# Two ranked expert lists with If/Else arms, two dense blocks, and one-hots with two tokens innermost

## The chip, the core and the metric

One core of a Trainium2 chip runs the whole program. The metric is the device time of one execution in microseconds; a kernel's time is the median of its runs.

## The reference

Two layers of a network on 256 tokens of width 2048 (an S5 mixer, sparse attention, then a block with two linear-attention mixers), and at the end the part that matters here, a layer of 16,384 small experts. Each token picks, for each of 8 heads, the 16 best experts; every expert e has a row u_e and a row v_e of 2048 numbers:

```python
expert = i1 * 128 + i2                      # 8 heads x 16 picks for a token
gate = softmax(best)                        # over the 16 of a head
hid = gelu(sum_d x[t, d] * u[expert, d])
y[t] = sum over the 128 picks of gate * hid * v[expert]
h = h + y; out = rmsnorm(h) * final_norm_g
```

## The kernel before

Everything below is in `peer`, the last stage, and the generators that it drives, `gates` and `sort`. Tokens are two halves of 128, t = 0 and 1. An expert's index is n1 * 128 + p: n1 is one of 128 blocks, p a partition. The kernel computes the hidden value of all experts for all tokens, multiplies it by a gate that is zero where a token did not pick the expert, and multiplies only those experts by v that some token picked.

**The `pu` loop.** For each n1, 48 matmuls of 128 x 256 give the 128 experts' hidden values for 256 tokens (`mm_b`, line 212). The weights come in two units of 512 KB for each n1; ACT rounds a unit to its high part (`wh`, line 152) and DVE takes the rest (`wl`, line 153), three units ahead. A gelu (line 1741) and a DMA on ACT's queue write 128 rows of `WG` in memory (line 1742); a row of `WG` holds one expert's 256 hidden values, then its 256 gates.

**`gates`** runs through a hook between the matmuls of that loop, from n1 = 32. For four tokens at a time (`build`), DVE makes one-hots: `gA` (which p), `gE` (which n1) and `gB` (gE times the three bf16 parts of the gate). Sixteen bf16 matmuls of 128 columns turn them into gates (`pg`, line 1529) and into counts for each expert and half (`cnt`, line 1530). ACT copies the result to `gst`, and every 64 tokens 8 DMAs from ACT's queue write the gates to `WG` (line 1536). **`sort`** follows through the same hook: it classes each expert as picked in both halves, the first only, the second only, or neither, gives each a position in this order by prefix sums, and turns the positions into a list of expert numbers, again with one-hots and matmuls of 256 columns (`pL`, line 1615). The list lies as `idx`, 128 positions of 128 experts; `cuts` holds the ends of the classes in positions.

**The visits** (lines 1777 to 1811). 128 positions are taken in an order fixed by hand. A position is guarded by registers that hold the cuts: what lies behind the end is skipped by every engine. In a visit POOL gathers 128 rows of v (`vraw`, 1 MB, line 1721) and 128 rows of `WG` (`wg`, 256 KB, line 1729) by indirect DMA, each in a guard of its own, up to four and three visits ahead. POOL multiplies hidden value and gate (`hm`, line 1786), ACT rounds (`hh`, `vwh`, lines 1787 and 1789), DVE takes the rests (`hlo`, `vwl`, lines 1788 and 1790). TensorE adds three products of such parts to the 2048 output columns of a half, 12 matmuls of 512 columns for each half that the position serves (`mm`, line 1799): one half for the classes first and second, two for both. Zero matmuls (line 1774) clear the accumulators beforehand. The tile framework orders each engine's instructions, so a call that stands later in the text can stand earlier on an engine.

The **final norm** (lines 1814 to 1829) adds the accumulators to h on DVE, squares on ACT, takes the root on POOL (line 606), scales and writes out.

Of the kernel before, what the change touches and what calls it, by code (L numbers as in the profile page):

```python
# [169 lines left out]
class Kern:  # L170
# [1325 lines left out]
    def gates(self, P, RT, G, cnt):  # L1496
# [7 lines left out]
        def build(b):  # L1504
            ts = slice(b * nt, (b + 1) * nt)
            A = P.tile([128, 128, nt], BF16, name="gA", bufs=2)
            E = P.tile([128, 128, nt], BF16, name="gE", bufs=2)
            B = P.tile([128, 3, 128, nt], BF16, name="gB", bufs=2)
            bc = lambda n: RT[:, n, None, ts].to_broadcast([128, 128, nt])
            v.tensor_tensor(A, self.iota4, bc(1), op=OP.is_equal)  # L1510
            v.tensor_tensor(E, self.iota4, bc(0), op=OP.is_equal)
            v.tensor_tensor(B, E[:, None, :, :].to_broadcast([128, 3, 128, nt]),
                            RT[:, 2:5, None, ts].to_broadcast([128, 3, 128, nt]), op=OP.mult)
            AB[b] = A, E, B

        build(0)
        yield 1
        for b in range(T // nt):
# [4 lines left out]
            if b * nt % ng == 0:  # L1523
                st = self.stage.tile([128, 128, ng], F32, name="gst", bufs=2)
            ps = self.psum.tile([128, nt, 128], F32, tag="g", name="pg", bufs=2)
            half, first, last = b * nt // 128, b * nt % 128 == 0, (b + 1) * nt % 128 == 0
            for j in range(nt):
                for n in range(3):
                    pe.matmul(ps[:, j, :], A[:, :, j], B[:, n, :, j], start=(n == 0), stop=(n == 2))
                pe.matmul(cnt[:, half, :], A[:, :, j], E[:, :, j], start=(first and j == 0), stop=(last and j == nt - 1))  # L1530
            o = b * nt % ng
            act.activation(st[:, :, o:o + nt], ps.rearrange("p t n -> p n t"), AF.Copy)
            if o + nt == ng:
                for n in range(0, 128, 16):
                    t0 = b * nt + nt - ng
                    nc.scalar.dma_start(G[n * 128:(n + 16) * 128, t0:t0 + ng].rearrange("(n p) t -> p n t", p=128),
                                        st[:, n:n + 16, :])
            yield 1

    def sort(self, P, cnt, idx, cuts):  # L1540
# [7 lines left out]
        v.tensor_scalar(m, cnt, 1.0, None, op0=OP.min)  # L1548
        I = tl([4, 128], "sI")
# [3 lines left out]
        v.tensor_scalar(I[:, 3], m[:, 0], -1.0, 1.0, op0=OP.mult, op1=OP.add)  # L1553
        yield 1
        S = tl([4, 128], "sS")
        fl = lambda x: x.rearrange("p a b -> p (a b)")
        v.tensor_tensor_scan(fl(S), fl(self.smask), fl(I), 0.0, op0=OP.mult, op1=OP.add)
        R = tl([4], "sR")
        v.tensor_copy(R, S[:, :, 127])
        ps = self.psum.tile([128, 2, 4], F32, tag="g", name="psr", bufs=2)  # L1560
# [3 lines left out]
        tot, cum, off = tl([4], "stot"), tl([4], "scum"), tl([4], "soff")  # L1564
        v.tensor_copy(tot, ps[:, 1])
        v.tensor_tensor_scan(cum, self.ones[:, 0:4], tot, 0.0, op0=OP.mult, op1=OP.add)
        v.tensor_tensor(off, cum, tot, op=OP.subtract)
        v.tensor_tensor(off, off, ps[:, 0], op=OP.add)
        v.tensor_scalar(off, off, -1.0, None, op0=OP.add)
        ci = tl([4], "sci", I32)  # L1570
        v.tensor_copy(ci[:, 0:3], cum[:, 0:3])
        v.tensor_copy(ci[:, 3:4], cum[:, 2:3])
        v.tensor_scalar(cuts[:, 0:2], ci[:, 0:2], 127, None, op0=OP.add)
        v.tensor_copy(cuts[:, 2:3], ci[:, 1:2])
        v.tensor_scalar(cuts[:, 3:4], ci[:, 3:4], 127, None, op0=OP.add)
        v.tensor_scalar(cuts, cuts, 7, None, op0=OP.arith_shift_right)
        yield 1
        for c in range(4):
            v.scalar_tensor_tensor(S[:, c], S[:, c], off[:, c:c + 1], I[:, c], op0=OP.add, op1=OP.mult)
        pos = tl([128], "spos")  # L1580
        v.tensor_reduce(pos, S.rearrange("p c n -> p n c"), axis=AX.X, op=OP.add)
# [13 lines left out]
        def build(b):  # L1595
            ts = slice(b * nt, (b + 1) * nt)
            A = P.tile([128, 128, nt], BF16, name="gA", bufs=2)
            E = P.tile([128, 128, nt], BF16, name="gE", bufs=2)
            B = P.tile([128, 3, 128, nt], BF16, name="gB", bufs=2)
            for o, a in ((A, 0), (E, 1)):  # L1600
                v.tensor_tensor(o, self.iota4, pb[:, a, None, ts].to_broadcast([128, 128, nt]), op=OP.is_equal)
            v.tensor_tensor(B[:, 0:2], E[:, None, :, :].to_broadcast([128, 2, 128, nt]),
                            self.nv[:, :, None, ts].to_broadcast([128, 2, 128, nt]), op=OP.mult)
            AB[b] = A, B
# [12 lines left out]
        Ls = tl([2, 128], "sL")  # L1617
        v.tensor_copy(Ls, L)
        v.scalar_tensor_tensor(idx, Ls[:, 0], 128.0, Ls[:, 1], op0=OP.mult, op1=OP.add)
        yield 1  # L1620

    def peer(self, keep, M, mixR, g1):
# [63 lines left out]
        self.iota4 = rt([128, 4], "iota4", BF16)  # L1686
        v.tensor_copy(self.iota4, ib[:, :, None].to_broadcast([128, 128, 4]))
        self.srt, self.ones, self.smask = rt([129], "srt"), rt([128], "ones"), rt([4, 128], "smask")
# [3 lines left out]
        v.tensor_copy(self.nv[:, 1], self.srt[:, 128:129].to_broadcast([128, 128]))  # L1692
        gp.memset(self.ones, 1.0)
        gp.memset(self.smask, 1.0)
        gp.memset(self.smask[:, :, 0:1], 0.0)
# [3 lines left out]
        idx = rt([128], "idx", U32)  # L1699
        cuts = rt([4], "cuts", I32)  # L1700
        WG = self.dram.tile([16384, 2 * T], F32, name="WG")
        left, stage = ExitStack(), ExitStack()
        NR, NS, NV = 32, 78, 54
        reg = {}

        def regs():
            for k, n, engines in (("both", 0, (ET.PE,)), ("first", 1, (ET.PE,)), ("second", 2, (ET.PE,)),
                                  ("end", 3, (ET.PE,)), ("load", 3, (ET.Pool,)),
                                  ("split", 3, (ET.Activation, ET.DVE, ET.Pool))):
                reg[k] = nc.values_load(cuts[0:1, n:n + 1], engines=engines, min_val=0, max_val=128)  # L1710


        order = [j for n in range(NV) for j in (n, n + NV)] + list(range(2 * NV, 128))
        raw, wg, hl = {}, {}, {}

        def gather_v(q):
            if q < 128:
                j = order[q]
# [5 lines left out]
        def gather_w(q):  # L1724
            if q < 128:
                j = order[q]
                wg[q] = vr.tile([128, 2, T], F32, name="wg", bufs=4)
                with tc.If(reg["load"] > j):
# [4 lines left out]
        for n in range(128):  # L1733
# [17 lines left out]
            elif n == 123:  # L1751
                self.finish()
                regs()
                for q in range(4):
                    gather_v(q)
# [14 lines left out]
        for q in range(3):  # L1770
            gather_w(q)
# [118 lines left out]
```

## Time and profile before

| | |
|---|---|
| median of 3 runs | 3229.49 us (3229.22 to 3232.59) |
| profiled execution: its own time, its span | 3227.61 us, 3225.7 us |
| mean granted TensorE clock | 0.958 of full speed |
| TensorE, DVE, ACT, POOL busy | 91%, 59%, 43%, 21% |
| `pu` matmuls, line 212, x6144 | 758.0 + 583.5 us busy |
| products of the visits, line 1799, x1920 | 257.9 + 252.8 + 251.3 us busy |
| gathers on POOL, x109 each | 178.8 us (`wg`) and 171.3 us (`vraw`) |
| hm on POOL, hlo and vwl on DVE | x109 each; vwl 249.6 us |

The busy times of matmuls overlap, so the time of a product is read from starts. The page's chain of waits breaks off at POOL's queue near the end; what stands there is read from the timeline and the waits. The stages of the whole: other layers until 1669 us, the `pu` loop to 2606, the visits to 3125, the final norm to 3225.7.

### The profile page before, as it was taken

To read this page: it belongs to the slowest core of one execution; us is meant where nothing else is said; L and a number is where in the kernel's file an instruction comes from. 1 tells how busy PE (TensorE), PEld (TensorE's weight loads), DVE (VectorE), ACT (ScalarE), POOL (GpSimd) and SP (SyncE) were. 2 spreads that over 40 slices of the span, in tenths; PEclk is the share of its full clock that TensorE was granted. 3 is DMA by queue.
4 is the path that set the end of the run, shared out by engine and by line. 5 is a ranking of instruction groups with operands and counts; after the bars stand their busy time and mean duration, and the time that the engine had idled before them with its cause. 6 is when DMAs were issued, how large, how long until landed. Compare 5 with 4: busy or idle time off the path is not lost. (4 is left out here: it accounts for less than half of the span.)

```text
span 3225.7 us, 51109 instructions
## 1 busy us (share of the span) xinstructions
PE 2944.7 (91%) x19491; PEld 2668.9 (83%) x19496; DVE 1895.3 (59%) x2632; ACT 1376.7 (43%) x1806; POOL 677.7 (21%) x502
## 2 busy tenths in 40 slices
PE   7888999999997999899999999999899989999950
PEld 6887899888787999788899999999799967777740
DVE  8858544555567663575689855555654445555540
ACT  4464333444445573444434433334234434444430
POOL 4443000000001000310001100000000048878840
PEclk9889999999998999999999999999899999999985
DMA  4244645444564553236656656655666668878840
GB/s 166 66 143 160 215 165 176 138 144 142 172 224 145 174 158 107 69 113 221 193 174 194 197 154 177 176 157 155 178 221 207 206 216 292 292 277 283 288 162 26
DMA packets 216662, 574.38 MB, mean 178 GB/s; under 512 B 84240, under 2 KB 101776, under 8 KB 200144
## 3 DMA queue, kind: packets, MB, share of 16 engines
q1 hardware_dynamic: 106928, 392.32, 37.8%
q0 software_dynamic: 24416, 142.88, 12.4%
q10 hardware_dynamic: 85056, 35.66, 4.0%
q8 instruction: 167, 2.74, 0.3%
q14 instruction: 95, 0.78, 0.1%
HBM read 530.95 MB, written 39.85 MB: 177 GB/s over the span
## 5 line engine op out<-in xcount | busy, mean ns | idle before, releaser
L153 DVE TENSOR_TENSOR wl<-raw,wh 128x1024 fp32r<-128x1024 f32 x685 | 885.8, 1296 | 790.3 <-ACT wh L152 785.7
L152 ACT ACTIVATE wh<-raw 128x1024 fp32r<-128x1024 f32 x688 | 728.7, 1060 | 1156.0 <-PE pu L212 385.0
L212 PE MATMUL pu<-h,wh 128*128 128x256 f32 x4096 | 758.0, 286 | 6.8 <-ACT wh L152 5.5
L212 PEld LDWEIGHTS pu<-h,wh 128*128 128x128 f32 x4096 | 641.9, 191 | 10.0 <-ACT wh L152 5.9
L212 PE MATMUL pu<-h,wl 128*128 128x256 f32 x2048 | 583.5, 285 | 5.4 <-DVE wl L153 5.1
L212 PEld LDWEIGHTS pu<-h,wl 128*128 128x128 f32 x2048 | 388.0, 189 | 8.2 <-DVE wl L153 8.1
L227 PE MATMUL pz<-wh,t 128*128 128x512 f32 x1024 | 336.0, 400 | 0.0
L1790 DVE TENSOR_TENSOR vwl<-vraw,vwh 128x2048 fp32r<-128x2048 f32 x109 | 249.6, 2290 | 103.6 <-ACT vwh L1789 103.6
L1799 PE MATMUL acc<-vwh,hh 128*128 128x512 f32 x640 | 257.9, 403 | 57.1 <-PEq L1807 18.8
L1799 PE MATMUL acc<-vwh,hlo 128*128 128x512 f32 x640 | 252.8, 395 | 0.0
L1799 PE MATMUL acc<-vwl,hh 128*128 128x512 f32 x640 | 251.3, 393 | 0.0
L1729 POOL DMA_INDIRECT wg<-WG,idx x109 | 178.8, 1640 | 259.0 <-DMA WG<-w 233.6
L227 PEld LDWEIGHTS pz<-wh,t 128*128 128x128 f32 x1024 | 192.4, 188 | 40.7 <-issue 1.0
L1789 ACT ACTIVATE vwh<-vraw 128x2048 fp32r<-128x2048 f32 x109 | 208.3, 1911 | 18.4 <-PE acc L1799 11.7
L1799 PEld LDWEIGHTS acc<-vwh,hh 128*128 128x128 f32 x640 | 121.0, 189 | 107.0 <-ACT hh L1787 46.0
L227 PE MATMUL pz<-wl,t 128*128 128x512 f32 x512 | 201.2, 393 | 1.6 <-DVE wl L153 1.4
L227 PE MATMUL pso<-wh,t 128*128 128x512 f32 x640 | 200.6, 393 | 0.3 <-DVE th L986 0.3
L1721 POOL DMA_INDIRECT vraw<-pv,idx x109 | 171.3, 1571 | 136.7 <-PE pu L212 96.0
L1787 ACT ACTIVATE hh<-hm 128x256 fp32r<-128x256 f32 x109 | 44.6, 409 | 253.2 <-POOL hm L1786 253.2
L1799 PEld LDWEIGHTS acc<-vwh,hlo 128*128 128x128 f32 x640 | 121.1, 189 | 30.7 <-DVE hlo L1788 5.3
L227 PEld LDWEIGHTS pso<-wh,t 128*128 128x128 f32 x640 | 120.2, 188 | 27.1 <-DVE th L986 0.7
L1799 PEld LDWEIGHTS acc<-vwl,hh 128*128 128x128 f32 x640 | 121.2, 189 | 23.0
(601 smaller groups left out, 5150.5 us busy)
## 6 DMA issues: line engine op xcount, KB each, us to landing
raw<-pu SPq DMA_DIRECT2D x256, 512.0 KB, 3.8
raw<-w_z SPq DMA_DIRECT2D x96, 512.0 KB, 3.4
raw<-w_fqi SPq DMA_DIRECT2D x48, 512.0 KB, 3.5
raw<-w_a_in SPq DMA_DIRECT2D x32, 512.0 KB, 3.5
raw<-w_q SPq DMA_DIRECT2D x32, 512.0 KB, 3.4
raw<-w_b_out SPq DMA_DIRECT2D x32, 512.0 KB, 4.0
raw<-w_conv SPq DMA_DIRECT2D x32, 512.0 KB, 3.7
raw<-w_gz SPq DMA_DIRECT2D x32, 512.0 KB, 3.4
```

The source lines that it names most:

```text
L152: self.nc.scalar.activation(h, t, AF.Copy)
L153: m = (engine or self.nc.vector).tensor_tensor(l, t, h.bitcast(F32), op=OP.subtract).ins
L212: mm = nc.tensor.matmul(ps, a[:, c], b(k), start=(k == 0 and n == 0), stop=(k == nk - 1 and n == len(ops) - 1))
L227: self.nc.tensor.matmul(pss[tt], x[a](k)[:, ts], b[:, kk * 512:(kk + 1) * 512], start=(k == 0 and n == 0), stop=(k == nk - 1 and n == 2))
L1721: gp.indirect_dma_start(out=raw[q], out_offset=None, in_=i["pv"], in_offset=bass.IndirectOffsetOnAxis(ap=idx[:, j:j + 1], axis=0))
L1729: gp.indirect_dma_start(out=wg[q].rearrange("p a t -> p (a t)"), out_offset=None, in_=WG[:, :], in_offset=bass.IndirectOffsetOnAxis(ap=idx ...
L1787: act.activation(hh, hm, AF.Copy)
L1789: act.activation(wh, r, AF.Copy)
L1790: v.tensor_tensor(wl, r, wh.bitcast(F32), op=OP.subtract)
L1799: pe.matmul(acc[t][e], a[:, ts], b[:, es], start=False, stop=True, skip_group_check=True)
```

## The change

`gates` and `sort` hold one-hots as [2 groups, 128, 2 tokens] instead of [128, 4 tokens], so a matmul reads every second element instead of every fourth; gB is built by two DVE instructions instead of one. `sort` makes two lists. List 1 (a = 0) holds the experts of both halves, then those of the first only; list 2 (a = 1) holds those of the second only, its chunks numbered on from the end of class both or from position 44, whichever is later. A position n is one visit: the list-1 chunk serves the first half; then an If/Else adds to the second half either the same chunk (class both) or list 2's chunk n. Positions 0 to 81 are taken in a merged order of the first 50 and the other 32; a second loop over the rest stands behind a guard that is true only if a list is longer than 82 positions. List 2 gathers only the second half of a row of `WG`, which now holds [half, hidden or gate, 128 tokens] behind one row of zeros. The last two n1 blocks (126, 127) are left out of the lists: their v rows are loaded whole at n1 = 118 and 119, and each is multiplied for both halves; the first of them starts the accumulators in place of the zero matmuls. Both gathers of a job stand in one guard, three jobs ahead; `hm` is on DVE; `vraw` has 3 buffers instead of 4. The registers are read at n1 = 116 instead of 123.

The diff, cut to what moves work (`self.split` is the ACT copy and the DVE subtraction of the visits):

```diff
 def gates
+    def hot(self, P, name, vals, parts=1):
+        o = P.tile([128, 2, 128, 2], BF16, name=name, bufs=2)
+        self.nc.vector.tensor_tensor(o, self.iota2[:, None, :, :].to_broadcast([128, 2, 128, 2]),
+                                     vals.rearrange("p (g i) -> p g i", i=2)[:, :, None, :].to_broadcast([128, 2, 128, 2]),
+                                     op=OP.is_equal)
+        return o
...
-            v.tensor_tensor(A, self.iota4, bc(1), op=OP.is_equal)
-            v.tensor_tensor(E, self.iota4, bc(0), op=OP.is_equal)
-            v.tensor_tensor(B, E[:, None, :, :].to_broadcast([128, 3, 128, nt]),
-                            RT[:, 2:5, None, ts].to_broadcast([128, 3, 128, nt]), op=OP.mult)
+            A, E = self.hot(P, "gA", RT[:, 1, ts]), self.hot(P, "gE", RT[:, 0, ts])
+            B = P.tile([128, 3, 2, 128, 2], BF16, name="gB", bufs=2)
+            for g in range(2):
+                tg = slice(b * nt + 2 * g, b * nt + 2 * g + 2)
+                v.tensor_tensor(B[:, :, g], E[:, None, g].to_broadcast([128, 3, 128, 2]),
+                                RT[:, 2:5, None, tg].to_broadcast([128, 3, 128, 2]), op=OP.mult)
...
-                    pe.matmul(ps[:, j, :], A[:, :, j], B[:, n, :, j], start=(n == 0), stop=(n == 2))
+                    pe.matmul(ps[:, j, :], A[:, g, :, k], B[:, n, g, :, k], start=(n == 0), stop=(n == 2))
...
-                for n in range(0, 128, 16):
+                for n in range(0, nn, nn // 7):
...
+                nc.scalar.dma_start(GD[:, half, t0:t0 + ng].rearrange("(n p) t -> p n t", p=128), st[:, nn:128, :])
 def sort
-                pe.matmul(L, A[:, :, j], B[:, 0:2, :, j], start=(b + j == 0), stop=(b == nb - 1 and j == nt - 1))
+                pe.matmul(L, A[:, g, :, k], B[:, 0:2, g, :, k], start=(b + j == 0), stop=(b == nb - 1 and j == nt - 1))
 def peer
+        NR, ND, NQ0, NM = 32, 2, 44, 82
...
-        order = [j for n in range(NV) for j in (n, n + NV)] + list(range(2 * NV, 128))
+        order = sorted(range(NM), key=lambda n: (n + 0.5) / 50 if n < 50 else (n - 49.5) / (NM - 50))
...
+        def cond(r, a, n):
+            both, first, second = reg[r]
+            return (first > n) if a == 0 else (both <= n) & (second > n)
+
+        def jobs(ns):
+            return [(a, n) for n in ns for a in range(2) if (n >= NQ0 if a else n < 128)]
...
-                raw[q] = vr.tile([128, D], F32, name="vraw", bufs=4)
-                with tc.If(reg["load"] > j):
-                    gp.indirect_dma_start(out=raw[q], out_offset=None, in_=i["pv"],
-                                          in_offset=bass.IndirectOffsetOnAxis(ap=idx[:, j:j + 1], axis=0))
+            r = raw[job] = vr.tile([128, D], F32, name="vraw", bufs=3)
+            g = wg[job] = vr.tile([128, 2 - a, 2, 128], F32, name=f"wg{a}", bufs=3)
...
+            with tc.If(cond("load", a, n)):
+                gp.indirect_dma_start(out=g.rearrange("p a b t -> p (a b t)"), out_offset=None,
+                                      in_=wghalf if a else wgrows, in_offset=off(0))
+                gp.indirect_dma_start(out=r, out_offset=None, in_=i["pv"], in_offset=off(1))
...
-                gp.tensor_tensor(hm, g[:, 0], g[:, 1], op=OP.mult)
+            with tc.If(cond("split", a, n)):
+                v.tensor_tensor(h, g[:, :, 0], g[:, :, 1], op=OP.mult)
...
+            with tc.If(first > n):
+                mm(w[0], 0)
+            with tc.If(both > n) as c:
+                mm(w[0], 1, 1)
+            if 1 in w:
+                with c.Else():
+                    with tc.If(second > n):
+                        mm(w[1], 1)
...
+                for x, (f, ahead) in enumerate(((gather, 3), (gate, 2), (prep, 1))):
...
-            nc.scalar.dma_start(WG[n * 128:(n + 1) * 128, 0:T], w)
+            if n < nn:
+                nc.scalar.dma_start(WG[1 + n * 128:129 + n * 128, :, 0, :], w)
+            else:
+                wh, wl, hh, hlo, g = dense[n]
+                h = vs.tile([128, 2, 128], F32, name="hm0", bufs=3)
+                v.tensor_tensor(h, w, g, op=OP.mult)
+                self.split(hh, hlo, h)
...
+            elif 118 <= n < 118 + ND:
+                m = nn + n - 118
+                r = vr.tile([128, D], F32, name="vraw", bufs=3)
+                nc.sync.dma_start(r, i["pv"][m * 128:(m + 1) * 128])
...
+                self.split(wh, wl, r)
...
-        for t in range(2):
-            for e in range(4):
-                pe.matmul(acc[t][e], z[:, 0:128], z, start=True, stop=True)
+        for n in range(nn, 128):
+            for t in range(2):
+                mm(dense[n][0:4], t, t, n == nn)
+        run(order)
+        with tc.If(reg["all"] > NM):
+            run(range(NM, NQ0 + 128))
```

Two places where the order of instructions moves. The first is DVE at the end of the `pu` loop. Before, in this order (`wl` is a weight unit's rest, the guard of line 1785 is that of the first visit):

```order
L153 TENSOR_TENSOR wl<-raw,wh 128x1024
L1619 SCALAR_TENSOR_TENSOR idx<-sL 128x128
L1720 UNCONDITIONAL_BRANCH x4
L153 TENSOR_TENSOR wl<-raw,wh 128x1024 x77
L1728 UNCONDITIONAL_BRANCH x2
L1710 TENSOR_LOAD cuts
L1785 COMPARE_AND_BRANCH
L1790 TENSOR_TENSOR vwl<-vraw,vwh 128x2048
L1788 TENSOR_TENSOR hlo<-hm,hh 128x256
```

and after the change (`hm_25361`, `hlo_25422` and `vwl_25420` belong to the first job of list 2, `hm_25194` and `hm_25249` to the dense blocks; line 1758 is a gather's guard, 1767 the guard of hm, 1778 that of the splits):

```order
L1767 COMPARE_AND_BRANCH
L1768 TENSOR_TENSOR hm_25361<-wg_25331 128x128
L1767 UNCONDITIONAL_BRANCH x2
L1778 ISA
L1778 REGISTER_ALU
L1778 COMPARE_AND_BRANCH
L177 TENSOR_TENSOR hlo_25422<-hm_25361,hh_25421 128x128
L177 TENSOR_TENSOR vwl_25420<-vraw,vwh_25419 128x2048
L1778 UNCONDITIONAL_BRANCH x2
L1758 UNCONDITIONAL_BRANCH
L153 TENSOR_TENSOR wl<-raw,wh 128x1024
L1838 TENSOR_TENSOR hm_25194<-w,gd 128x256
```

The last weight unit's rest, which before had no instruction of the visits ahead of it, now stands behind hm, hlo and vwl of a gathered chunk.

The second is POOL in the visits. Before, each gather and each hm stands in a guard of its own; the row ISA is what runs where the guard skips:

```order
L1720 COMPARE_AND_BRANCH
L1721 DMA vraw<-pv,idx 128x2048
L1720 UNCONDITIONAL_BRANCH
L1720 ISA
L1720 UNCONDITIONAL_BRANCH
L1785 COMPARE_AND_BRANCH
L1786 TENSOR_TENSOR hm<-wg 128x256
L1785 UNCONDITIONAL_BRANCH x2
L1785 COMPARE_AND_BRANCH
L1786 TENSOR_TENSOR hm<-wg 128x256
L1785 UNCONDITIONAL_BRANCH x2
```

and after the change, one job:

```order
L1758 COMPARE_AND_BRANCH
L1759 DMA wg_27556<-WG,idx 128x512
L1761 DMA vraw<-pv,idx 128x2048
L1758 UNCONDITIONAL_BRANCH
L1758 ISA
L1758 UNCONDITIONAL_BRANCH
```

The two gathers share a guard and a single ISA row, and the two hm between them are gone from POOL.

## Rows read from the trace of the kernel before

**Rows 1.** windows of the `pu` loop and the visits; busy us (count), clock, DMA share

```profile
2000.00:2050.00 50.00, 50.00 (x421) 49.36 (x420) 28.22 (x39) 18.74 (x26) 0.00 (x0) 1.00 0.47 143
...
2700.00:2750.00 50.00, 47.01 (x202) 37.34 (x201) 29.76 (x23) 22.71 (x22) 44.08 (x34) 1.00 0.82 290
```

**Rows 2.** timeline of the span's end; start us, duration us, engine, line, operation

```profile
3124.82 0.63 PE L1799 MATMUL acc<-vwh,hlo 128*128 128x512 f32 x1
...
3141.82 3.68 DVE L1818 TENSOR_TENSOR h<-h,acc 128x512 f32<-128x512 f32 x6 [20.50 <-PEq L1807]
...
3208.70 0.56 POOL L606 TENSOR_TENSOR ssf<-rs_a,mhalf 128x1 f32<-128x1 f32 x1 [88.30 <-POOLq L1785]
...
3217.30 0.38 SPq L1829 DMA_DIRECT2D out<-h  x1
```

**Rows 3.** instructions of line 1720, the guard of the v gather, on POOL's queue

```profile
L1720 POOLq INC_SWDGE_SEM  x19: 2382/2382/2389, 3105.7 to 3205.2; - x19
```

**Rows 4.** timeline, one-hot and zero matmuls on PE

```profile
2255.54 0.52 PE L1529 MATMUL pg<-gB,gA 128*128 128x128 bf16 x3
...
2257.31 0.29 PE L1530 MATMUL cnt<-gE,gA 128*128 128x128 bf16 x1
...
2271.01 2.00 PE L1615 MATMUL pL<-gB,gA 128*128 128x256 bf16 x8 [4.33 <-DVE gE L1601]
...
2607.00 1.89 PE L1774 MATMUL acc<-zero 128*128 128x512 bf16 x7 [0.47 <-ACT w L1741]
```

**Rows 5.** DVE's one-hot builds, by tile; duration ns min/median/max, first and last start

```profile
L1510 DVE TENSOR_TENSOR gA<-iota,rt x64: 404/418/426, 1733.2 to 2248.3; 128x512 bf16<-128x512 bf16 x64
...
L1512 DVE TENSOR_TENSOR gB<-gE,rt x64: 943/958/964, 1735.6 to 2249.1; 128x1536 bf16<-128x1536 bf16 x64
```

**Rows 6.** waits from 1960 to 2000 us, around one gst write; us in total, times, longest

```profile
ACT wh L152 <- DMA WG<-gst: 17.8, 1, 17.8
...
PE pu L212 <- ACT wh L152: 5.5, 1, 5.5
```

**Rows 7.** timeline of the `pu` loop's end

```profile
2596.29 0.33 ACTq L1742 DMA_DIRECT2D WG<-w  x1
...
2616.39 0.95 POOL L1729 DMA_INDIRECT wg<-WG,idx  x1 [233.63 <-DMA WG<-w]
...
2621.05 0.80 PE L1799 MATMUL acc<-vwh,hh 128*128 128x512 f32 x1 [12.17 <-ACT hh L1787]
```

**Rows 8.** DMA issues; count, KB each, median us from issue to landing

```profile
WG<-w ACTq DMA_DIRECT2D x128, 128.0 KB, 2.5
...
vraw<-pv,idx POOLq DMA_INDIRECT x109, 7.6
```

**Rows 9.** costliest groups of the page; busy us, mean ns | idle before, releaser

```profile
L1799 PE MATMUL acc<-vwh,hh 128*128 128x512 f32 x640 | 257.9, 403 | 57.1 <-PEq L1807 18.8
...
L1729 POOL DMA_INDIRECT wg<-WG,idx x109 | 178.8, 1640 | 259.0 <-DMA WG<-w 233.6
...
L1721 POOL DMA_INDIRECT vraw<-pv,idx x109 | 171.3, 1571 | 136.7 <-PE pu L212 96.0
```

**Rows 10.** instructions of line 1786 on POOL; duration ns min/median/max

```profile
L1786 POOL TENSOR_TENSOR hm<-wg x109: 719/747/1102, 2619.8 to 3119.7; 128x256 f32<-128x256 f32 x109
```

**Rows 11.** timeline of two visits, 2697 to 2703 us

```profile
2697.88 0.95 POOL L1721 DMA_INDIRECT vraw<-pv,idx  x1 [0.30 <-issue]
...
2698.32 2.29 DVE L1790 TENSOR_TENSOR vwl<-vraw,vwh 128x2048 fp32r<-128x2048 f32 x1 [1.61 <-ACT vwh L1789]
...
2698.49 1.91 ACT L1789 ACTIVATE vwh<-vraw 128x2048 fp32r<-128x2048 f32 x1
...
2699.13 2.30 POOL L1729 DMA_INDIRECT wg<-WG,idx  x1 [0.30 <-issue]
...
2699.81 0.39 PE L1799 MATMUL acc<-vwl,hh 128*128 128x512 f32 x1
...
2702.30 0.39 PE L1799 MATMUL acc<-vwh,hh 128*128 128x512 f32 x1
```

More of the change, by code (lines that the diff above doesn't have):

```diff
@@ L1527, in gates @@
             for j in range(nt):
+                g, k = j // 2, j % 2
                 for n in range(3):
-                    pe.matmul(ps[:, j, :], A[:, :, j], B[:, n, :, j], start=(n == 0), stop=(n == 2))
-                pe.matmul(cnt[:, half, :], A[:, :, j], E[:, :, j], start=(first and j == 0), stop=(last and j == nt - 1))
+                    pe.matmul(ps[:, j, :], A[:, g, :, k], B[:, n, g, :, k], start=(n == 0), stop=(n == 2))
+                pe.matmul(cnt[:, half, :], A[:, g, :, k], E[:, g, :, k], start=(first and j == 0),
+                          stop=(last and j == nt - 1))
             o = b * nt % ng
@@ L1582, in sort @@
+        for n in range(3):
+            v.tensor_tensor(pos, pos, S[:, n], op=OP.add)
         pi = tl([128], "spi", I32)
@@ L1702, in peer @@
+        gp.memset(zrow, 0.0)
+        nc.sync.dma_start(WG[0:1], zrow)
+        wgrows, wghalf = WG.rearrange("r a b t -> r (a b t)"), WG.rearrange("r a b t -> (r a) (b t)")
         left, stage = ExitStack(), ExitStack()
-        NR, NS, NV = 32, 78, 54
         reg = {}
         def regs():
[L1707 to L1710, printed above, removed]
@@ L1724, in gather_w @@
[L1724 to L1728, printed above, removed]
[L1729 to L1732 removed]
+            for name, engines in (("pe", (ET.PE,)), ("split", (ET.Activation, ET.DVE)), ("load", (ET.Pool,))):
+                reg[name] = [nc.values_load(cuts[0:1, n:n + 1], engines=engines, min_val=0, max_val=256) for n in (0, 1, 3)]
@@ new lines, in gate, with tiles @@
+        def gate(job):
+            a, n = job
+            h = hm[job] = vs.tile([128, 2 - a, 128], F32, name=f"hm{a}", bufs=3)
+            g = wg.pop(job)
+            with tc.If(cond("split", a, n)):
+                v.tensor_tensor(h, g[:, :, 0], g[:, :, 1], op=OP.mult)
+        def tiles(a):
+            w = [vs.tile([128, D], F32R, name=f"{x}{a}", bufs=3 - a) for x in ("vwh", "vwl")]
+            return w + [vs.tile([128, 2 - a, 128], F32R, name=f"{x}{a}", bufs=3 - a) for x in ("hh", "hlo")]
@@ new lines, in prep, with mm @@
+        def prep(job):
+            a, n = job
+            wh, wl, hh, hlo = vt[job] = tiles(a)
+            r, h = raw.pop(job), hm.pop(job)
+            with tc.If(cond("split", a, n)):
+                self.split(hh, hlo, h)
+                self.split(wh, wl, r)
+        def mm(w, t, k=0, start=False):
+            wh, wl, hh, hlo = w
+            for e in range(4):
+                es = slice(e * 512, (e + 1) * 512)
+                for n, (a, b) in enumerate(((hh, wh), (hh, wl), (hlo, wh))):
+                    pe.matmul(acc[t][e], a[:, k], b[:, es], start=start and n == 0, stop=True, skip_group_check=True)
@@ new lines, in visit @@
+        def visit(n):
+            w = {a: vt.pop((a, n)) for a, n in jobs([n])}
+            both, first, second = reg["pe"]
+            if 0 not in w:
+                with tc.If(second > n):
+                    mm(w[1], 1)
+                return
+            with tc.If(first > n):
[4 more added lines that the diff above has]
+                with c.Else():
+                    with tc.If(second > n):
+                        mm(w[1], 1)
@@ new lines, in run, with upto @@
+        def run(ns):
+            js = jobs(ns)
+            at = {j: k for k, j in enumerate(js)}
+            done = [0, 0, 0]
+            def upto(k):
+                for x, (f, ahead) in enumerate(((gather, 3), (gate, 2), (prep, 1))):
+                    while done[x] < min(len(js), k + ahead):
+                        f(js[done[x]])
+                        done[x] += 1
+            upto(0)
+            for n in ns:
+                for j in jobs([n]):
+                    upto(at[j] + 1)
+                visit(n)
@@ L1793, in mm @@
[L1793 to L1812 removed]
+        acc = {t: [self.psum.tile([128, 512], F32, name=f"acc{t}{e}") for e in range(4)] for t in (1, 0)}
```

187 lines of the change are left out of this document (83 added, 104 removed).

## The prediction

> **What bounds the kernel now.** I read the busy shares by stretch first, then the end of the span, then the stage that the change rewrites. In the loop of `pu` blocks TensorE is busy all of the time at full clock (50.00 of 50 us, 421 matmuls) while POOL does nothing; in the visits TensorE still has 47.01 of 50, but POOL has 44.08 as well, and gaps between its instructions fill most of the rest [rows 1]. At the end nothing computes: the last matmul ends at 3124.82 + 0.63 = 3125.45, DVE's first addition of the final norm starts at 3141.82 after TensorE's queue has walked the remaining guards, and the next step, a tiny POOL instruction, starts at 3208.70 after 88.3 us of waiting for POOL's own queue [rows 2]. So POOL's queue bounds the last 83 us. What it does there is one instruction type: a skipped guard on a gather runs a semaphore increment of 2382 ns, 19 for each of the two gathers, the last at 3205.2 [rows 3]. 38 of them on 19 visits make the tail. I call the end of the last `pu` matmul E0: the zero matmuls start at 2607.00 after 0.47 of idle, so E0 = 2606.5 [rows 4]. From there to the span's end, 3225.7, are 619.2 us.
>
> **The one-hots.** In `gates` TensorE reads gA, gE and gB with a step of 4 elements. The 16 matmuls of a block start between 2255.54 and 2257.31, so 15 steps in 1.77 us, 0.118 us for 128 columns; 8 pL matmuls of 256 columns take 2.00 us, about 0.227 each; the contiguous bf16 zero matmuls need 1.89 us for 7 of 512 columns, about 0.25 each once the first is in [rows 4]. That is 0.89 to 0.92 ns a column against 0.49. After the change the step is 2 elements. No row shows that step; the bounds are the two paces. I take 0.063 us per 128 and 0.126 per 256 columns, because the slow pace is so close to a factor of two that it reads like one fetch doing half of its work, and two tokens innermost halves the step. 1024 matmuls (768 pg, 256 cnt) times 0.055 are 56 us, 128 pL times 0.10 are 13: 69 us, all on the path, as TensorE has no idle time there [rows 1]. The Trainium skill speaks against this part: its page "SBUF — State Buffer", in the box on cachelines under "Door 1: The DMA port swizzle", holds that two accesses to a 16-byte line give full bandwidth, so a bf16 step of 4 would already be free and this term zero. The two paces above disagree with it, and the sum goes by them.
>
> Some of it comes back. Four times ACT issues 8 gst DMAs in one go; its weight split then waits 17.8 us for them and TensorE 5.5 us [rows 6]. A faster TensorE uses up the three split units of cover 2 to 2.7 us earlier, in each of four: +8. DVE pays nothing that shows: A and E keep 512 elements (0.418), B becomes two instructions of 768, by the slope between 512 and 1536 elements (0.418 and 0.958) 0.55 each instead of one of 0.96 [rows 5], +0.15 in a block whose TensorE work is near 5 us. Even at twice the price per element (+3.3 a block) DVE only draws level with TensorE. One-hots: **-61** (bounds -75 and +8).
>
> **Edits at nothing.** Each n1 block of v that stays dense is loaded on SP's queue and split by ACT and DVE (1.91 and 2.29, as in the visits [rows 11]) in the blocks 118 and 119. Three split units of cover, each 24 matmuls of 0.119 [rows 1], 8.6 us in all, hide them; without it the two cost 5. The gst writes stay 8 in each of four, the sort's small DVE work and the memsets lie under TensorE's loop.
>
> **The loop's end.** The new order puts, on DVE, hm, hlo and vwl of the first job of list 2 ahead of the last weight split `wl`, and on ACT its hh and vwh ahead of a gelu. So half of `pu` block 127 waits for a gather: behind the waiting hm stand `wl` and the two dense hm on DVE, and TensorE waits for all three. The gathers wait for the gates of n1 = 125, whose write is issued at 2596.29 [rows 7] and lands 2.5 later [rows 8]: 2598.8. Then six gathers of about 1.25 on POOL (2606.3), 7.6 to land [rows 8] (2613.9), about 5 for the split, 1.2 for `wl`, 3.5 for 24 matmuls, some at half clock: 2623.6. I take **+18** (0 if the data lands early; 24 if the 3 MB of `h` loads, which slowed the last write until 2616.39 [rows 7], slow these gathers too). Before, the same place holds 14.5 us between E0 and the first product at 2621.05 [rows 7], which go with it.
>
> **The visits.** Before: 3 x 640 matmuls [rows 9] are 160 products of 12, and 11 starts from 2699.81 to 2702.30 are 2.49 us [rows 11], so 2.72 a product, 435 of the 504 us from 2621.05 to 3125.45. After, by the reference's own routing of its inputs without the last 256 experts: list 1 has 78 chunks, 50 of which serve both halves, list 2 has 29. That is 78 + 50 + 29 = 157 products, **427**, and four dense ones, **11**; the zero matmuls go.
>
> Does POOL keep up? A gather that meets no DVE instruction takes 0.95; one that starts while vwl runs (2698.32 to 2700.61) takes 2.30 and ends 0.82 after vwl does [rows 11]. The means are 1.571 and 1.640 [rows 9]; hm is 0.75 [rows 10]. Before, a visit costs POOL 1.57 + 1.64 + 0.75 and three gaps of 0.30, 4.9, and TensorE 160 / 109 x 2.72 = 4.0: POOL set the pace. After, hm is on DVE (about 0.43, as gA of the same size [rows 5]) and one guard holds both gathers: 1.57 + 1.64 + 0.6 = 3.81 for 107 jobs, 408, under TensorE's 427. Buffers: vraw has 3 instead of 4, and each is held from issue over 7.6 of landing [rows 8], 1.91 of vwh and 2.29 of vwl [rows 11], some 12 us, so one job per 4.0, just what TensorE uses. DVE needs about 3.15 a job. With three resources within 5% of TensorE, waits are certain: I take **25** (0 to 55; the upper end is a little above what was lost before per job, 0.6 x 107 = 64, less hm).
>
> **Skips and tail.** The order has 82 positions of list 1 and 38 of list 2, 120 jobs, 107 of them real. 13 skips stay, all in the last tenth. One skip instruction now serves both gathers: 13 x (2.38 + 0.27 for guard and branch) = 34 us on POOL, mixed with some 7 real jobs. TensorE is up to three jobs behind POOL there, so about half shows: **18** (0 to 34). The loop behind it (list over 82) isn't taken; its skip is one instruction on POOL that raises eight counters, taken at 2.4 like the others. After it the rest is as before: 4.4 from the first addition to POOL's step (six additions of 0.61, a reduce, a scale) and 3225.7 - 3208.7 = 17 from there [rows 2], less what overlaps, **20** from the last matmul (15 to 30).
>
> **Sum.** 18 + 11 + 427 + 25 + 18 + 20 = 519 against 619: -100, with the one-hots -161. The profiled execution has a span of 3225.7 and a time of 3227.6, the median of the runs is 3229.5, 1.9 above it. 3229.5 - 161 = **3069**.
>
> **Rivals.**
> *One-hots bring nothing* (the fetch is no better at a step of 2; or DVE falls behind): 61 to 64 us stay, **3133**. For it: no row shows the step of 2. Against: the clean factor of two. 0.12. It is also what the cacheline rule of the Trainium skill, cited above, would give.
> *Visits keep their pace*: the third buffer or the shorter lookahead costs what moving hm saves; 107 x (504 / 109) = 495 in place of 452, +42, **3111**. 0.11.
> *DVE and POOL never overlap*: every gather waits for DVE and DVE for every gather, 329 + 107 x 2 x 0.95 = 532 in place of 452, **3149**. Against: the same sum for before, 296 + 288 = 584, is over the 504 seen, and vwl is 2.29 whether or not a gather stands beside it [rows 11]. 0.04. The Trainium skill's page "SBUF — State Buffer", section "SBUF: two separate sides", states such a lock between a DVE instruction with two SBUF inputs and GpSimd, for whichever starts first; the rows bear out the half in which POOL waits.
> *Slower*: a skip's 2382 ns is the price per amount added, not per instruction. The skip of the loop behind adds, for all of its jobs, 34 times the amount to each of eight counters: 272 x 2.38 = 647 us on POOL, ahead of the final norm, **3716**. It decides from 161 us on. For it: 2382 is long for one write and constant to 1.6%. Against: a single instruction with its amount as an operand. 0.05.
> *The fallback runs*: if a list were longer than 82 after all, 136 more jobs, nearly all skips of 2.65, 360 us: **3430**. Against: 78 and 79 by the counts. 0.02.
> The rest, 0.04: the order at the loop's end and the skips both cost nothing, under 3035.
>
> **Numbers.** The forecast holds 0.62, between 3030 and 3105. The range reaches to 3140 to take in the two likelier rivals, and to 3025 below: that holds 0.85 or a little less. A change of 0.2%, 6.5 us, is about the least that a measurement of this kernel tells from none. Faster by more: 0.62 + 0.12 + 0.11 + 0.04 + 0.04 = 0.93, of which I take one point for mixtures that end near zero; slower 0.07.
>
> **What would show it.** Rows of pg near 0.063 us a start, and some 470 or more matmuls in windows of the loop that has 421; a wait of `pu` for `wl` or of DVE for a gather at the loop's end, 13 to 19 us; visits that end some 480 us after E0 with POOL under 90% busy; 13 increments and one more instead of 38, POOL's step of the final norm within 10 us of the last matmul. Wrong is this if the increments are longer than 2.4 us, if pg keeps 0.118, or if products come every 4.6 us a job.

## The result and the profile after

The changed kernel takes 3110.91 us, the median of 4 runs, beside 3229.35 us for the kernel before: a ratio of 0.9644, 95% interval 0.9615 to 0.9673. That is 118 us less; the forecast was 161 less (3069), with a range of 3025 to 3140. The profiled execution has a span of 3109.6 us.

The end of the span is what was forecast. The timeline (start us, duration us) answers to [rows 2]:

```profile
3089.46 0.39 PE L1787 MATMUL acc<-vwh,hlo 128*128 128x512 f32 x1
...
3089.98 3.68 DVE L1887 TENSOR_TENSOR h<-h,acc 128x512 f32<-128x512 f32 x6 [7.24 <-PEq L1880]
...
3096.46 0.56 POOL L606 TENSOR_TENSOR ssf<-rs_a,mhalf 128x1 f32<-128x1 f32 x1
...
3101.47 0.38 SPq L1898 DMA_DIRECT2D out<-h  x1
```

From the start of the last matmul to the end are 20.1 us, where before they were 100.9, and POOL's small step comes 6.6 us after the last matmul instead of 83. The increments left on POOL's queue are 13 at the gathers' guard (line 1758) and one for the whole loop that is not taken (line 1880), against 38 [rows 3]; count, duration ns min/median/max, first and last start:

```profile
L1758 POOLq INC_SWDGE_SEM  x13: 2080/2227/2321, 3015.4 to 3072.1; - x13
...
L1880 POOLq INC_SWDGE_SEM  x1: 2318/2318/2318, 3078.6 to 3078.6; - x1
```

The groups of the page that answer to [rows 9] (busy us, mean ns, idle before): a gather is shorter on average by 0.2 to 0.3 us, and vwl is what it was:

```profile
L177 DVE TENSOR_TENSOR vwl<-vraw,vwh 128x2048 fp32r<-128x2048 f32 x109 | 249.7, 2292 | 101.7 <-ACT vwh L176 79.9
...
L1759 POOL DMA_INDIRECT wg<-WG,idx x107 | 144.4, 1350 | 766.2 <-ACT wh L152 699.4
...
L1761 POOL DMA_INDIRECT vraw<-pv,idx x107 | 148.2, 1385 | 173.6 <-issue 79.1
```

The one-hot matmuls of a block now start at 0.058 us (2185.54 to 2186.41 are 15 steps), half of the 0.118 of [rows 4]; the builds of gB are two of 0.55 us on DVE, as worked out from [rows 5]:

```profile
2185.54 0.35 PE L1536 MATMUL pg<-gB,gA 128*128 128x128 bf16 x3
...
2186.41 0.22 PE L1537 MATMUL cnt<-gE,gA 128*128 128x128 bf16 x1
```

At the end of the `pu` loop the wait that the order announced is there. In the timeline hm of list 2's first job waits 18.25 us for its gather, `wl` stands behind it, and TensorE waits 20.33 us; after that its first matmuls run at the lower of its two clocks, 1.2 instead of 2.4 GHz (0.58 us for one that takes 0.28 else; the mean granted clock is 0.68 in the 4.6 us from 2564.4 and 1.00 from 2569 on). The first dense product follows the last `pu` matmul at once, where [rows 7] have a gap of 14.5 us:

```profile
2555.71 0.29 DVE L1768 TENSOR_TENSOR hm<-wg 128x128 f32<-128x128 f32 x1 [18.25 <-DMA wg<-WG,idx]
...
2563.15 1.22 DVE L153 TENSOR_TENSOR wl<-raw,wh 128x1024 fp32r<-128x1024 f32 x1
...
2564.42 0.58 PE L212 MATMUL pu<-h,wl 128*128 128x256 f32 x1 [20.33 <-DVE wl L153]
...
2569.10 0.47 PE L1787 MATMUL acc<-vwh,hh 128*128 128x512 f32 x1 [0.52 <-issue]
```

In the visits the windows (busy us of PE, PEld, DVE, ACT, POOL, clock, DMA share, GB/s) answer to the second of [rows 1]: POOL is no longer near 90%, yet TensorE is busy less (43.61 of 50 against 47.01). This stretch is one of the worst: from 2700 to 3000 us TensorE is busy 269.7 us, against 278.7 in the kernel before. In the last 60 us, where the skipped guards stand, it is busy for half of the time and its granted clock falls to 0.74.

```profile
2700.00:2750.00 50.00, 43.61 (x187) 34.52 (x187) 33.28 (x35) 24.19 (x22) 32.31 (x23) 1.00 0.80 294
...
3050.00:3110.00 60.00, 29.43 (x96) 21.80 (x96) 19.52 (x24) 14.18 (x24) 10.27 (x10) 0.74 0.27 97
```

The waits from 2620 to 2990 us name vwl for TensorE, vwh for vwl, and the v gather's landing for vwh; the longest in total is another, that of hh for hm, which is on DVE now (us in total, times, longest):

```profile
ACT hh L176 <- DVE hm L1768: 66.2, 25, 4.6
DVE vwl L177 <- ACT vwh L176: 60.7, 61, 2.8
...
ACT vwh L176 <- DMA vraw<-pv,idx: 54.5, 41, 3.3
...
PE acc L1787 <- DVE vwl L177: 31.9, 29, 2.3
```

**Where the time went.** The stages of both kernels and of the experiments, from the first and last starts of the `pu`, pL and acc matmuls in the tile views (visits: first to last acc matmul; tail: from there to the span's end). The first `pu` matmul starts between 1664.6 and 1672.4 us in all these runs, though the program up to it is the same in all of them, so a single profile has some 4 us of such noise and the columns start behind it. Two such rows, of the changed kernel and of the same without skips:

```profile
L1787 PE MATMUL acc<-vwh,hlo x644: 387/389/632, 2569.6 to 3089.5; 128*128 128x512 f32 x161
```

```profile
L1787 PE MATMUL acc<-vwh,hlo x644: 387/389/628, 2573.4 to 3067.6; 128*128 128x512 f32 x161
```

| kernel | median us | first pu to last pL | last pL to last pu | to first product | visits | tail |
|---|---|---|---|---|---|---|
| before | 3229.4 | 704.6 | 232.7 | 14.8 | 503.8 | 100.9 |
| changed | 3110.9 | 650.9 | 252.2 | 0.8 | 520.4 | 20.1 |
| before, new one-hots | 3166.6 | 644.1 | 231.6 | 14.5 | 504.1 | 100.7 |
| changed, old one-hots | 3176.7 | 708.0 | 252.7 | 0.8 | 521.1 | 20.1 |
| before, 109 positions | 3145.0 | 704.5 | 233.3 | 14.6 | 499.7 | 18.2 |
| changed, no skips | 3091.7 | 650.1 | 252.7 | 0.9 | 494.7 | 20.1 |
| changed, list 2 later | 3107.4 | 650.9 | 230.4 | 0.8 | 523.1 | 27.4 |
| both of these | 3090.7 | 650.8 | 230.4 | 0.8 | 511.5 | 20.5 |
| changed, v gathers of half the bytes | 3094.0 | 650.0 | 250.6 | 0.8 | 490.5 | 20.1 |
| changed, 4 v buffers | 3127.2 | 649.9 | 252.6 | 0.9 | 529.0 | 21.1 |
| changed, list 2 in one buffer | 3120.9 | 652.3 | 252.1 | 0.8 | 524.0 | 20.1 |
| changed, hm on POOL | 3204.4 | 650.7 | 252.2 | 0.8 | 605.8 | 20.1 |
| before, v gathers of half the bytes | 3226.3 | 704.7 | 230.5 | 14.7 | 503.9 | 100.6 |
| no skips, list 2 later, 4 v buffers | 3082.8 | 651.8 | 230.4 | 2.8 | 504.6 | 20.4 |

The tail gives 81 us and the loop with the one-hots 54; the loop's end takes 20 and gives back 14, and the visits take 17 more. They have 161 products, 437 us at the products' pace (1931 steps of 0.2265 us), and 83 us above it.

### The profile page after: what moved, and what is told of

It is laid out like the page before. It is cut to its first block, busy times and chain, and to the rows that moved or that the text cites. A ratio compares the mean times of both kernels' runs of the same rounds, so it can differ in the third digit from the quotient of the medians.

```text
span 3109.6 us, 50843 instructions
## 1 busy us (share of the span) xinstructions
PE 2879.5 (93%) x19496; PEld 2619.3 (84%) x19500; DVE 1933.3 (62%) x2846; ACT 1370.7 (44%) x1806; POOL 537.7 (17%) x391
## 5 line engine op out<-in xcount | busy, mean ns | idle before, releaser
L212 PE MATMUL pu<-h,wh 128*128 128x256 f32 x4096 | 754.8, 286 | 11.5 <-ACT wh L152 10.2
L212 PE MATMUL pu<-h,wl 128*128 128x256 f32 x2048 | 581.1, 284 | 25.9 <-DVE wl L153 25.7
L1787 PE MATMUL acc<-vwl,hh 128*128 128x512 f32 x644 | 262.1, 407 | 43.5 <-DVE vwl L177 36.2
L1759 POOL DMA_INDIRECT wg<-WG,idx x107 | 144.4, 1350 | 766.2 <-ACT wh L152 699.4
L1761 POOL DMA_INDIRECT vraw<-pv,idx x107 | 148.2, 1385 | 173.6 <-issue 79.1
L176 ACT ACTIVATE hh<-hm 128x256 fp32r<-128x256 f32 (+1 forms) x109 | 41.9, 385 | 220.6 <-DVE hm L1768 101.5
```

The costliest lines, as they stand in the source:

```text
L176: self.nc.scalar.activation(h, x, AF.Copy)
L212: mm = nc.tensor.matmul(ps, a[:, c], b(k), start=(k == 0 and n == 0), stop=(k == nk - 1 and n == len(ops) - 1))
L1759: gp.indirect_dma_start(out=g.rearrange("p a b t -> p (a b t)"), out_offset=None, in_=wghalf if a else wgrows, in_offset=off(0))
L1761: gp.indirect_dma_start(out=r, out_offset=None, in_=i["pv"], in_offset=off(1))
L1787: pe.matmul(acc[t][e], a[:, k], b[:, es], start=start and n == 0, stop=True, skip_group_check=True)
```

## The experiments

**The one-hots alone.** The kernel before with only this edit, and the changed kernel with it undone:

```diff
-            A = P.tile([128, 128, nt], BF16, name="gA", bufs=2)
+            A, E = self.hot(P, "gA", RT[:, 1, ts]), self.hot(P, "gE", RT[:, 0, ts])
-                    pe.matmul(ps[:, j, :], A[:, :, j], B[:, n, :, j], start=(n == 0), stop=(n == 2))
+                    pe.matmul(ps[:, j, :], A[:, g, :, k], B[:, n, g, :, k], start=(n == 0), stop=(n == 2))
```

> The kernel before with the two-token one-hots alone; lists, visits and order stay. If the one-hots are what moved the end of the pL matmuls by 54 us in the changed kernel, the loop's end moves by as much here: 3229 - 54 = 3175, range 3168 to 3185, and the visits keep their 504 us. Rival: part of those 54 us came from the other edits in the loop (dense blocks not written, other gst writes); then this kernel gains under 40: 3190 or more.

> The changed kernel with the old one-hots of four tokens, everything else as changed. If the parts add up, it loses what the one-hots gave: 3111 + 54 = 3165, range 3155 to 3175, and pg goes back to 0.118 us a start. Rival: the slower loop hides the wait at the loop's end or the gst holds, so less comes back: 3135 to 3150.

Measured: 3166.57 us, ratio 0.9808 (0.9792 to 0.9824), and 3176.74 us, ratio 0.9833 (0.9814 to 0.9853). Alone the one-hots shorten the loop by 60.5 us, in the changed kernel by 57.1, and a start of pg goes from 0.118 to 0.058 us and back. The parts add up. Both medians lie just outside the expected ranges, on the side of a larger effect, by less than the noise in front of the loop. The rival, that other edits did it, falls; those cost 3.4 us in this stretch (708.0 against 704.6).

**The skips.** In the kernel before the loop of visits is cut to the real positions; in the changed kernel two constants take 12 of the 13 skipped jobs out of the program.

```diff
-        for q in range(128):
+        for q in range(109):
...
-        NR, ND, NQ0, NM = 32, 2, 44, 82
+        NR, ND, NQ0, NM = 32, 2, 50, 79
```

> The kernel before with the loop of visits cut to the 109 positions that are real for these inputs (the guards stay, the 19 skipped positions are not in the program). If the tail of 100 us is the skips' increments on POOL, 78 to 82 us go: 3147 to 3152, with the last matmul where it was. Rival: DVE's and ACT's part of the tail (20 us of waiting for TensorE's queue and the norm itself) stays long: only 60 to 70 us go, 3160 to 3170.

> The changed kernel with list 2 numbered from 50 and a loop of 79 positions: 12 of the 13 skipped jobs are not in the program, the real jobs are the same. If the increments of 2.1 to 2.3 us on POOL's queue make the slow end of the visits (28 us over the products' pace in the last 70 us, against 8 us in a like stretch before), about 18 us go: 3093, range 3087 to 3099. Rival: the slow end is the draining of the last gathers and stays: 3105 or more.

Measured: 3144.98 us, ratio 0.9733 (0.9715 to 0.9751), and 3091.73 us, ratio 0.9575 (0.9552 to 0.9597). Before, the tail falls from 100.9 to 18.2 us and POOL's step starts in time:

```profile
3123.91 0.56 POOL L606 TENSOR_TENSOR ssf<-rs_a,mhalf 128x1 f32<-128x1 f32 x1 [10.65 <-DVE rs_a L604]
```

So the increments were the tail, and more than half of what the change gains could have been had by ending the loop at the last real position. In the changed kernel the visits shorten by 25.7 us without them.

**The loop's end.** List 2's chunks come three steps later in the merged order, so that neither DVE nor ACT holds one of its jobs before the last weight unit; then the same without skips.

```diff
-        order = sorted(range(NM), key=lambda n: (n + 0.5) / 50 if n < 50 else (n - 49.5) / (NM - 50))
+        order = sorted(range(NM), key=lambda n: (n + 0.5) / 50 if n < 50 else (n - 49.5 + 3) / (NM - 50))
```

> The changed kernel with list 2's chunks three steps later in the merged order, so that no guard of a gathered chunk stands before the last weight split on DVE or before a gelu on ACT. If the wait of 20.3 us in the last pu block comes from that order alone, it goes, and the first chunks have landed when the four dense products (11 us) are done: 15 to 19 us less, 3092 to 3096. Rival: the wait only moves to the first gathered product, as in the kernel before (14.5 us between the loop and the first product): 3106 to 3111.

> The changed kernel with both edits: no skipped jobs (list 2 from 50, 79 positions) and list 2 three steps later in the order. The order alone moved the loop's end by 21 us but put skips behind the last product (tail 27 instead of 20 us). Without skips that tail has no cause: 3092 less 18 to 21, 3071 to 3075. Rival: the visits lose what the loop gains, since they start before the first chunks are there: 3085 to 3092.

Measured: 3107.44 us, ratio 0.9619 (0.9598 to 0.9640), and 3090.65 us, ratio 0.9564 (0.9547 to 0.9581). The wait of 20 us is gone in both (252 to 230 us), and most of the time is not: against 3110.91 and 3091.73 the medians differ by 3.5 and 1 us, less than the runs of one kernel scatter; counted from the first `pu` matmul, the profiled executions are 12 and 5 us shorter. Without skips the visits take 16.8 us more than with the old order. About half of that stands in their first 50 us, which hold 167 matmuls instead of 205, as TensorE now waits for the first gathered chunks (from the version without skips):

```profile
2572.48 0.79 PE L1787 MATMUL acc<-vwl,hh 128*128 128x512 f32 x1 [7.81 <-DVE vwl L177]
```

The stream of v gathers keeps its time: counted from the first `pu` matmul, the first starts at 875.1 us with the old order and 876.4 with the new one, the fourth at 897.7 and 889.2, the last at 1381.1 and 1379.5 (both without skips). So the order gains 8.5 us at the fourth gather and loses nearly all of it later. The wait was real and cost a few us, where 15 to 21 were expected.

**What sets the pace of the visits.** First the bytes, in both kernels: a v gather brings 1024 numbers of a row and the splits read them twice. (The row numbers stay, so in rows of half the length they point at parts of other experts' v; the number and the sizes of the instructions on ACT, DVE and TensorE stay as they were.)

```diff
-                gp.indirect_dma_start(out=r, out_offset=None, in_=i["pv"], in_offset=off(1))
+                gp.indirect_dma_start(out=r[:, 0:1024], out_offset=None, in_=i["pv"].rearrange("r (a d) -> (r a) d", a=2), in_offset=off(1))
...
-                self.split(wh, wl, r)
+                self.split(p3(wh), p3(wl), r[:, None, 0:1024].to_broadcast([128, 2, 1024]))
```

> The changed kernel with v gathers of half the bytes: each brings 1024 numbers a row, and the splits read them twice, so the instructions of ACT, DVE and TensorE keep their sizes (half of v is left out of the sums). If the transfers or their landing set the pace, by A or by B, the visits fall to TensorE's pace with the skips left: 35 to 50 us less, 3061 to 3076. Rival: the chain of DVE, ACT and POOL instructions sets it and the bytes are hidden: 3100 to 3111.

> The kernel before with v gathers of half the bytes, the splits reading them twice (half of v is left out of the sums). If POOL's queue sets the pace of its visits, the bytes are hidden: 3222 to 3232, visits 504 us. If transfers set it, the visits shorten as in the changed kernel with half the bytes (30 us): 3190 to 3205.

Measured: 3094.03 us, ratio 0.9569 (0.9548 to 0.9591), for the changed kernel, 3226.29 us, ratio 0.9997 (0.9988 to 1.0007), for the one before. Windows of 100 us, of the changed kernel, of it with half the bytes, and of the kernel before with half the bytes:

```profile
2700.00:2800.00 100.00, 90.83 (x383) 72.08 (x383) 66.11 (x67) 48.83 (x44) 62.72 (x45) 0.98 0.80 292
```

```profile
2700.00:2800.00 100.00, 95.02 (x411) 76.00 (x410) 68.67 (x71) 50.77 (x48) 71.81 (x47) 1.00 0.57 175
```

```profile
2700.00:2800.00 100.00, 93.60 (x401) 74.20 (x400) 58.77 (x45) 49.82 (x47) 87.59 (x67) 1.00 0.60 175
```

Before, halving the bytes changes nothing: the visits take 503.9 us with DMA engines far less busy. So bytes do not bound its visits, and instructions are left. Which engine's, this run does not tell; the waits of the kernel before, from 2640 to 3090 us, point at POOL, as the prediction did from its 44 of 50 us:

```profile
ACT hh L1787 <- POOL hm L1786: 215.3, 49, 5.6
```

No run takes hm off POOL in that kernel with all else the same. After the change half the bytes shorten the visits by 29.9 us, so a part of the bound has moved to the v rows' arrival. In the waits from 2620 to 2990 us vwh's for the v gather falls from 54.5 to 18.8 us, and hh's for hm stays:

```profile
ACT hh L176 <- DVE hm L1768: 65.0, 24, 3.2
...
ACT vwh L176 <- DMA vraw<-pv,idx: 18.8, 19, 2.2
```

Of the 6.3 us by which the products fall behind their pace in every 50 us from 2600 to 3000, 3.3 stay, so bytes are not all. (The changed kernel with half the bytes has runs of 3080, 3091 and 3097 us and one of 5674 that the median of 3094 counts; without it the median is 3091. The profiled one is the shortest.)

Then the buffers. The fourth v buffer needs room, which comes from list 2's split parts; a control has only that.

```diff
-            w = [vs.tile([128, D], F32R, name=f"{x}{a}", bufs=3 - a) for x in ("vwh", "vwl")]
+            w = [vs.tile([128, D], F32R, name=f"{x}{a}", bufs=3 - 2 * a) for x in ("vwh", "vwl")]
-            r = raw[job] = vr.tile([128, D], F32, name="vraw", bufs=3)
+            r = raw[job] = vr.tile([128, D], F32, name="vraw", bufs=4)
-                for x, (f, ahead) in enumerate(((gather, 3), (gate, 2), (prep, 1))):
+                for x, (f, ahead) in enumerate(((gather, 4), (gate, 2), (prep, 1))):
```

> The changed kernel with four buffers for the v rows again and gathers four jobs ahead; to make room, the tiles of list 2's split parts have one buffer instead of two. Theory A: the number of buffers sets the pace of the visits (a v gather is issued right after a vwl has freed its buffer); then most of the 55 us that the visits lose before the skips go, 25 to 40 us less: 3071 to 3086. Theory B: the transfers themselves set it (280 to 294 GB/s in both kernels), and one more buffer only lengthens the queue: 3103 to 3115.

> The changed kernel with list 2's split parts in one buffer instead of two and three v buffers as they are: the control for the version with four. If one buffer for list 2 is harmless, 3106 to 3116, and the fourth v buffer by itself costs 11 to 16 us. If it costs something itself, 3120 to 3135, and the fourth v buffer is worth nothing or a few us.

Measured: 3127.22 us, ratio 0.9679 (0.9660 to 0.9698), and the control 3120.89, ratio 0.9668 (0.9652 to 0.9684). The control costs something itself, and the fourth buffer adds 5 us of visits to it; the ratios' intervals overlap. Theory A, that the number of buffers sets the pace, does not hold: the v gathers that start from 2620 to 3000 us are 4.42 us apart with four buffers, 4.51 in the control and 4.50 in the changed kernel, where TensorE's own pace would be 4.0 (an estimate, 157 products of 2.72 us over 107 jobs), and the some 5 us that this gains over the control by then are lost again in the stretch of the skips. With three (changed kernel) or four, DMA moves 275 to 292 GB/s from 2600 to 3000 us. The kernel before moves 278 to 291 from 2700 on, and there half the bytes change nothing, so the rate alone does not show a bound.

Last hm, moved back to POOL with all else as changed.

```diff
-                v.tensor_tensor(h, g[:, :, 0], g[:, :, 1], op=OP.mult)
+                gp.tensor_tensor(h, g[:, :, 0], g[:, :, 1], op=OP.mult)
```

> The changed kernel with hm on POOL again instead of DVE. If POOL's queue set the pace of the visits before, as the prediction has it, it does so again: 1.38 + 1.35 + 0.75 and three gaps of 0.3 are 4.4 for a job before any added collisions, 4.9 with those of before: 15 to 35 us more, 3126 to 3146. If transfers set the pace in both kernels, moving hm costs nothing: 3105 to 3117.

Measured: 3204.40 us, ratio 0.9938 (0.9922 to 0.9955): 93 us worse, far more than either theory. The waits from 2650 to 3050 us, one hm beside a vwl (2804.85 to 2807.14), and a window of 100 us:

```profile
ACT hh L176 <- POOL hm L1768: 151.0, 35, 6.5
```

```profile
2804.85 2.29 DVE L177 TENSOR_TENSOR vwl<-vraw,vwh 128x2048 fp32r<-128x2048 f32 x1 [2.82 <-ACT vwh L176]
2805.26 2.46 POOL L1768 TENSOR_TENSOR hm<-wg 128x256 f32<-128x256 f32 x1 [1.74 <-ACT vwh L176]
```

```profile
2700.00:2800.00 100.00, 87.82 (x338) 67.93 (x337) 50.30 (x37) 40.23 (x36) 71.97 (x57) 0.91 0.64 237
```

POOL is busy 72 of 100 us there (the fifth number), so it is less its load than its order: hm of a near job stands behind gathers of later ones, hh waits for hm, and the splits behind hh free the buffers late. In the longest of these waits, 6.45 us before an hh at 2801.15, POOL runs three gathers in a row ahead of hm, the first of them 2.73 us long beside a vwl. That chain is read from the timeline and the waits; no run takes it apart. Some of the 93 us is the clock: from 2600 to 3100 us the granted clock is 0.91 and TensorE's busy time 0.260 us a matmul, in the changed kernel 0.99 and 0.236 from 2600 to 3000; over 1932 matmuls that is up to 45 us, an estimate.

**All together**: no skips, list 2 later, four v buffers.

> The changed kernel without skipped jobs (list 2 from 50, 79 positions), with list 2 three steps later and with four v buffers (list 2's split parts in one buffer). If transfers set the pace and the fourth buffer lost its 7 us of the steady part only in the stretch of the skips, this beats the version without skips a little: 3091 - 7 = 3084, range 3077 to 3090. If the buffers do set the pace and the skips hid it, the visits come near TensorE's pace: 3060 to 3070. If a longer queue of gathers harms by itself: 3095 or more.

Measured: 3082.80 us, ratio 0.9558 (0.9542 to 0.9574), the best version of these: 28 us under the changed kernel, of which 19 are the skips. It fits the reading by transfers and not the one by buffers. From the version with three v buffers (0.9564, 0.9547 to 0.9581) the ratios do not tell it apart.

## Why the prediction was right, and where it was off

The direction and the large terms held; the time came 42 us later than forecast, inside the range.

**The tail** was forecast at 20 us and is 20.1; the skip of the loop behind takes 2318 ns for eight counters, so the rival by which an increment is priced by its amount (647 us) is dead, as is the fallback.

**The one-hots** were forecast at -61: alone they give -60.5, in the changed kernel -57.1. The pace halves (0.118 to 0.058), so the cacheline rule of the Trainium skill ("SBUF — State Buffer", "Door 1: The DMA port swizzle"), by which a bf16 step of 4 elements is still free, does not hold for these operands: 0.118 us at a step of 4 and 0.058 at a step of 2 for 128 columns. The holds at the gst writes are there: the matmuls of pg wait 20.3 us for them instead of 11.9 and those of `pu` for wh 10.2 instead of 5.5, 13 us more where +8 was forecast. They also spoil the sign of 470 matmuls in 50 us: the window that had 421, 2000 to 2050 us, now has 410, with most of an 11.1 us hold in it, and one without a hold, 2150 to 2200 us, has 495.

**The loop's end** was forecast at +18 and the wait is 20.3. The step that failed is that I put it on the path. Without it the medians gain 3.5 and 1 us, since the stream of gathers behind it starts and, without skips, ends at the same time either way; I priced the wait against TensorE's chain alone.

**Skips**: forecast 18 of a possible 34, measured 25.7.

**The visits** are the step that failed by most: "with three resources within 5% of TensorE, waits are certain: I take 25". Without the skips they lose 57 us. That POOL set the pace before agrees with the runs and is not shown by one of its own: half the bytes gain nothing there, hh waits 215 us for POOL's hm, and hm back on POOL costs 93 us, by its order more than by its load. That it would then be TensorE's turn is not so: arrival of the v rows takes a part of POOL's place, worth some 24 us in the 400 us from 2600 on and 30 in all, with the skips in. The v gathers' mean step went only from 4.58 to 4.50 us, near the 4.6 that the prediction named as a sign of being wrong. The rival "visits keep their pace" had the better number here: it puts the gathered jobs at 495 us and the forecast at 452, and measured are 484 (494.7 without skips, less 11 for the dense products). That its total of 3111 is the measured time is luck, since it was 11 us too high there and the other terms were about as much too low. Its cause, the third buffer or the shorter lookahead, is not borne out: a fourth buffer, gathered four ahead, shortens the step by 2%, the visits not at all beside the control (529.0 and 524.0 us) and without skips by 7 us (504.6 and 511.5). What the rest of the 57 us hangs on stays open; of the waits that half the bytes leave as they were, the largest named is hh's for hm on DVE (66.2 and 65.0 us).

In sum, between the forecast span (3225.7 - 161 = 3064.7) and the measured one (3109.6): +32 from the visits' waits, +8 from the skips, +7 from the one-hots with the loop's other edits (-53.7 instead of -61), +2 from the loop's end, and -4 from the noise before the loop, 45.

## What to carry to other kernels

A skipped guard is not free when it skips an indirect DMA: here each costs 2.1 to 2.4 us on POOL's queue, and a fixed loop over data-dependent work should end where the work ends, by one outer guard. Ask of a wait on the compute path whether the longest chain runs through it; here most of a wait of 20 us hid behind a gather stream that takes as long either way. Moving work off the engine that sets the pace shows the next bound, so its price belongs in the sum (here the arrival of the v rows, worth 24 to 30 us), not only the busy shares of the engines.

## What was not expected of the hardware

The increment of a skipped gather costs about the same for one, two or eight counters (2382, 2227 and 2318 ns; the counters are read from the program) and, for the eight, with an amount 34 times as large. A POOL instruction of two SBUF inputs that starts while DVE's subtraction of 2048 columns runs lasts until just after that ends (hm 2.46 us instead of 0.75), while the subtraction keeps its 2.29; the Trainium skill's exclusive lock ("SBUF — State Buffer", "SBUF: two separate sides") describes POOL's side of it, against a POOL instruction that reads SBUF, as hm does. DVE can lose too, seldom: a subtraction that starts 0.26 us behind an hm, at 2820.22 in that kernel, takes 2.65 us, and the longest of 109 takes 2859 ns.
